# In-order ACT and DVE at the opening of the first feed-forward layer, and a new order of two tiles' steps

## The chip, the cores and the metric

The kernel runs on one core of a Trainium2 chip. The metric is the device time of one execution in microseconds (us). The core has a matrix engine (PE, with its weight loads shown apart as PEld), three engines for elementwise work (DVE, ACT, POOL) and SP, which issues the transfers. The engines run side by side. Each takes its own instructions in the order in which they were laid down, and they wait for each other by semaphores.

## The reference

One block works on 16 meta tokens and 1024 tokens of 1024 features in float32. A mixer (pooling and gated linear attention, merged by gates) is followed by a feed-forward part; what matters here is the end of the first and all of the second:

```
h = h + m @ w_out                                   # end of the mixer, m: the gated sum
u = rmsnorm(h, norm_ffn)
h = h + square(relu(u @ w_ff1)) @ w_ff2             # w_ff1: 1024 x 4096, w_ff2: 4096 x 1024
out = rmsnorm(h, norm_final)[:, 16:]
```

## The kernel before

**Products.** Every float32 operand is held as two float32r parts, high and low; a product is three matmuls (high x high, high x low, low x high: `mm3`, lines 246 to 248), each of 128 weights by 512 columns. The split of a weight block is a copy on ACT (L264, the high part) and a subtraction on DVE (L265, the low part), into one of four slots that go round.

**Quarters.** Both feed-forward layers save one product in eight by a Strassen scheme. In the first, `Quarters` takes the columns of `w_ff1` in 16 pairs of 128-column blocks. For pair i there are seven products, P1(i) to P7(i), each of four feature tiles by three matmuls, twelve matmuls in all. Their weights are blocks of `w_ff1` or sums of such blocks, made on DVE (`sums`, L315 for P5, L317 for P6, L319 for P7, L321 for P3); P1, P2 and P4 use blocks as they were loaded. Weights are made three products ahead of the product that uses them (`todo`); the blocks of pair i + 2 are loaded (L292) once P3(i)'s weights are made. The order of the products at the start is P1(0), P1(1), P2(0), P2(1), P5(0), P5(1), P6(0), P7(0), P4(0), P3(0), then P6(1), P1(2), P7(1), P5(2), P4(1), P2(2), P3(1) and so on (`order`). `run` is a generator: each step emits the weights three ahead, one product, and, after the next resume, what takes its result. P1 and P2 add into one bank of the `x` tag, whose copy after P1 is u2 (L361). P5 and P3 add into one bank of the `mm` tag; P6, P7 and P4 have an `ms` bank each. After P6, u2 is added (L369); after P7, u3 is made (L374) and the result A22 is taken from the P5 bank (L1494); P4 gives A12, and P3, added onto the P5 bank, gives A21. `ff_result` adds on DVE (L1494), then ACT does relu (L1496) and square (L1497), DVE forms sums (L1501 to L1509), and SP stores them (L1488).

**Moving operands.** The normalized tiles u, eight of 128 tokens, are transposed on PE and become seven operands. `turn_tile` does that for one tile: eight transposes into two banks, b[0] for the features 0 to 511 and b[1] for the rest (L1395). Tiles 0 to 3 give the operands of P1 and P2, and raw copies `lo` and `hi`, kept in `acc`. A tile t of 4 to 7 meets the copies of tile t - 4:

- `b12`, a copy of b[0] on ACT (L1404);
- `t1` = b[0] - lo on DVE (L1405), and its high part on ACT (L1406, `th`) and low part on DVE (L1407, `tl`): the operand of P5;
- both parts of b[1] (L1408, which calls L201 and L202): the operand of P3;
- lo = b[1] - t1, b12 = b[1] - b12, hi = hi - lo on DVE (L1409 to L1411), and both parts of the first two (L1414, L1415, tile `wo`): the operands of P6 and P7.

The operand of P4 is made of `hi` for all four column groups at once in `ff_room`: four copies on ACT (L1467, `t4h`) and four subtractions on DVE (L1468, `t4l`). After that `ff_room` gives the memory of `acc` to the results h.

**Order of the work.** `out_tile` multiplies one tile by a half of `w_out` in 24 matmuls, adds the residual (L1378), normalizes (`layer_norm`: ACT L234, L210, L212; DVE L211, L214, L218, L219, and L238, which writes u) and, between its two halves of matmuls, turns the tile of two steps earlier. The tiles come in the order 0, 4, 1, 5, 2, 3, 6, 7. So the last two, 6 and 7, are turned inside the first feed-forward layer, in `ff_layers`: tile 6 ahead of P1(1), tile 7 ahead of P2(1), and `ff_room` comes after P2(1). The first four weights are made ahead, in `ff_weights`.

PE's instructions keep the program's order throughout. Those of ACT, DVE and SP are placed by a scheduler that works with its own estimates of when operands are ready, except inside `in_order(True)` ... `in_order(False)`, where ACT's and DVE's keep the program's order among themselves. Instructions emitted outside such a section may still be placed between those inside. In the kernel before, such a section runs from the last part of the attention to `wo1_open`, ahead of `out_tile`; there is none in the stage of this change.

Of the kernel before, what the change touches and what calls it, by code (L numbers as in the profile page):

```python
# [11 lines left out]
ACT = mybir.ActivationFunctionType  # L12
ALU = mybir.AluOpType
# [92 lines left out]
def kernel(  # L106
# [10 lines left out]
    act, dve, pool, pe = nc.scalar, nc.vector, nc.gpsimd, nc.tensor  # L117
# [20 lines left out]
    def bank(tag):  # L138
        if tag in rota:
            turn_of[tag] = turn_of.get(tag, -1) + 1  # L140
            tag = rota[tag][turn_of[tag] % len(rota[tag])]
        return psp[tag].tile([P, 512], F32, name=f"b_{tag}", tag=tag)
# [48 lines left out]
    def f32(ap):  # L191
        return ap.bitcast(F32)
# [7 lines left out]
    def split_from_psum(hi, lo, ps):  # L200
        act.activation(hi, ps, ACT.Copy)  # L201
        dve.tensor_tensor(lo, ps, f32(hi), ALU.subtract)  # L202
# [47 lines left out]
    def quad(a):  # L250
        return a.rearrange("p (k c) -> p k c", k=4)
# [149 lines left out]
    S, rings = {}, [W1]  # L401

    def step(steps, fn, ring=None, aps=()):
        steps.append((ring, list(aps), fn))
# [38 lines left out]
    def halves():  # L443
        return [slice(h * HALF, (h + 1) * HALF) for h in range(2)]
# [28 lines left out]
    def v_tile(i, t, later=False):  # L473

        vw, w = S["vw"][i], 256 + 16 * (i == 0)
        if t == 8:
            half, at, n = 0, 0, META
        else:
            half, n = t // 4, P
            at = OFF[half] + (t % 4) * P  # L480
        b = bank("mm")[:n, :w]
        th, tl, hi, lo = TH[half][:, :, at : at + n], TL[half][:, :, at : at + n], vw[:, 0], vw[:, 1]
        if i == t == 0:

            for k in range(KT):
                pe.matmul(b, th[:, k], hi[:, k], start=k == 0, stop=False)
                pe.matmul(b, tl[:, k], hi[:, k], start=False, stop=False)
            for k in range(KT):
                pe.matmul(b, th[:, k], lo[:, k], start=False, stop=k == KT - 1)
        else:  # L490
            mm3(b, KT, lambda k: (th[:, k], tl[:, k]), lambda k: (hi[:, k], lo[:, k]))

        def leave():
            if t == 8:
                act.activation(vm[:, i * 256 : i * 256 + 256], b[:, :256], ACT.Copy)
            else:
                act.activation(S["v"][i][:, t], b[:, :256], ACT.Copy)

        def leave_lr():
            if i == 0:  # L500
                act.activation(S["lrtok"][:n, t], b[:, 256:], ACT.Copy)

        if later:
            return leave, leave_lr
        leave()
        leave_lr()
# [13 lines left out]
    def lr_turn():  # L520
        b = bank("ms")
        pe.transpose(b[:16, :16], S["lrtok"][:16, 8], ident[:16, :16])
        stacked(lrT_meta, b[:16, :16], 1)
        for h in range(2):
            b = bank("ms")
            for t in range(4):
                pe.transpose(b[:16, t * P : (t + 1) * P], S["lrtok"][:, 4 * h + t], ident)
            act.activation(gB[:16, h * HALF : (h + 1) * HALF], b[:16], ACT.Copy)
# [186 lines left out]
    def halved(p, j):  # L715

        h, l = gate_quarters.x[p] = [left.push(f"{p}{k}", [P, 4, HALF], F32R) for k in "hl"]
        for k in range(0, 4, 2):
            a = S["ut"][j][:, k : k + 2]
            act.activation(h[:, k : k + 2], a, ACT.Copy)  # L720
            dve.tensor_tensor(l[:, k : k + 2], a, f32(h[:, k : k + 2]), ALU.subtract)

    def differ(to, a, b):
        for k in range(0, 4, 2):
            to_, a_, b_ = (S["ut"][j][:, k : k + 2] for j in (to, a, b))
            dve.tensor_tensor(to_, a_, b_, ALU.subtract)

    def differences(run, values):


        b11, b21, b12, b22 = (0, 0), (0, 1), (1, 0), (1, 1)
        left.pop_to(S["left_x"])
        halved("P5", b11)
        for fn in values:
            fn()
        next(run)
        leave = v_tile(0, 8, True)
        differ(b11, b22, b11)
        next(run)
        for fn in leave:  # L740
            fn()
        halved("P6", b11)
        next(run)
        differ(b12, b22, b12)
        lr_turn()
        next(run)
        right.pop_to(S["right_ut"][4])
        halved("P7", b12)
        next(run)
        differ(b21, b21, b11)  # L750
        right.pop_to(S["right_ut"][2])
        halved("P4", b21)
        next(run)
        right.pop_to(S["right_ut"][0])
# [43 lines left out]
    one = []  # L798
# [212 lines left out]
    def in_order(on):  # L1011


        if on:
            S["order"] = tc.manual_schedule(engines={mybir.EngineType.Activation, mybir.EngineType.DVE})
            S["order"].__enter__()
        else:
            S.pop("order").__exit__(None, None, None)
# [344 lines left out]
    ORDER = (0, 4, 1, 5, 2, 3, 6, 7)  # L1363
# [18 lines left out]

        return fn

    def turn_tile(t, tags=("ms",)):

        u, acc, g = S["u2"][:, ORDER.index(t) % 2], S["acc"], t % 4
        cols, b = slice(g * P, (g + 1) * P), []  # L1390
        for j in range(2):
            turn_n[0] += 1
            b.append(quad(bank(tags[turn_n[0] % len(tags)])))
            for i in range(4):
                pe.transpose(b[j][:, i], u[:, (4 * j + i) * P : (4 * j + i + 1) * P], ident)  # L1395
        lo, hi = (quad(acc[:, g, c]) for c in halves())
        if t < 4:
            for j, raw_copy in enumerate((lo, hi)):
                k = slice(4 * j, 4 * j + 4)
                act.activation(raw_copy, b[j], ACT.Copy)  # L1400
                split_from_psum(MH[0][:, k, cols], ML[0][:, k, cols], b[j])
            return
        b12, t1 = (quad(acc[:, t, c]) for c in halves())
        act.activation(b12, b[0], ACT.Copy)  # L1404
        dve.tensor_tensor(t1, b[0], lo, ALU.subtract)  # L1405
        act.activation(MH[1][:, 0:4, cols], t1, ACT.Copy)  # L1406
        dve.tensor_tensor(ML[1][:, 0:4, cols], t1, f32(MH[1][:, 0:4, cols]), ALU.subtract)  # L1407
        split_from_psum(MH[1][:, 4:8, cols], ML[1][:, 4:8, cols], b[1])  # L1408
        dve.tensor_tensor(lo, b[1], t1, ALU.subtract)  # L1409
        dve.tensor_tensor(b12, b[1], b12, ALU.subtract)  # L1410
        dve.tensor_tensor(hi, hi, lo, ALU.subtract)  # L1411
        for n, a in enumerate((lo, b12)):
            fh, fl = (S["wo"][0][:, k, 4 * n : 4 * n + 4, cols] for k in range(2))
            act.activation(fh, a, ACT.Copy)  # L1414
            dve.tensor_tensor(fl, a, f32(fh), ALU.subtract)  # L1415

    for n, j in enumerate(YB[1]):
        if n < 2:
# [20 lines left out]
    for t in ORDER[:6]:  # L1439
        step(one, out_tile(t, 1))  # L1440
    step(one, lambda: ff_weights())
    for t in ORDER[6:]:
        step(one, out_tile(t, 1))

    def ff_weights():
        for n in range(4):
            ff_quarters.prime(n == 0)
        m = lambda half, j: tuple(t[half][:, 4 * j : 4 * j + 4] for t in (MH, ML))
        n = lambda j: tuple(S["wo"][0][:, k, 4 * j : 4 * j + 4] for k in range(2))
        ff_quarters.x = {"P1": m(0, 0), "P2": m(0, 1), "P5": m(1, 0), "P3": m(1, 1), "P6": n(0), "P7": n(1)}  # L1450
# [11 lines left out]
    def ff_room():  # L1462

        fh, fl = ff_quarters.x["P4"]
        for g in range(4):
            a, cols = quad(S["acc"][:, g, halves()[1]]), slice(g * P, (g + 1) * P)
            act.activation(fh[:, :, cols], a, ACT.Copy)  # L1467
            dve.tensor_tensor(fl[:, :, cols], a, f32(fh[:, :, cols]), ALU.subtract)  # L1468
        left.pop_to(S["left_acc"])
        S["h"] = left.push("h", [P, 2, 9, HALF], F32)  # L1470
        ff_quarters.room = True
# [165 lines left out]
    def ff_layers():  # L1637

        ff_open()
        del rota["mm"]  # L1640
        run = ff_quarters.run()
        for n in range(4):
            if n in (1, 3):
                turn_tile(ORDER[6 + n // 2])
            next(run)
        ff_room()
        for _ in run:
            pass

    for fn in (ff_layers, ff2_open, ff2):  # L1650
        step(one, fn)
# [47 lines left out]
```

## Time and profile before

| | us |
|---|---|
| median of 3 runs | 1238.97 (1238.19 to 1239.67) |
| the profiled execution, its own time | 1239.98 |
| span of its profile, first to last instruction | 1238.2 |
| first feed-forward layer, first to last product (about) | 617 to 930 of the span |

The page of the profile gives each engine's busy time, its share of the span and its count of instructions. A row of the timeline gives start, duration, engine, line, operation, output and inputs by the program's names, sizes and count; a bracket at its end gives the time that the engine sat idle before it and what released it. A row of the windows gives a stretch, its length and each engine's busy time with instruction counts, then the granted PE clock as a share of the full one, and the transfers. In the names, `b_mm`, `b_x` and `b_ms` are banks, `w1h` and `w1l` the parts of the weights, `th`, `tl`, `wo`, `t4h` and `t4l` parts of the moving operands. A queue of an engine is written with a q (SPq).

### The profile page before, as it was taken

What the parts mean: (1) busy time and instruction counts of PE and PEld (TensorE: products, weight loads), DVE (VectorE), ACT (ScalarE), POOL (GpSimd) and SP (SyncE); (2) the same over time, 40 slices, a digit from 0 to 9 for tenths busy, and PEclk for the clock granted to TensorE, in tenths of its full rate; (3) what the DMA queues carried; (4) which work ended last, traced back from release to release, by engine and by line L of the source; (5) the groups of instructions that cost most, each with busy time, mean ns of one, the idle gap of its engine ahead of it and who ended that gap; (6) DMA issues with size and microseconds to landing.
All of it is one profiled execution on the core that took longest, in us unless ns stands there. A gap on an engine that the chain in (4) does not pass through costs nothing.

```text
span 1238.2 us, 18288 instructions
## 1 busy us (share of the span) xinstructions
PE 1207.4 (98%) x6816; PEld 1006.6 (81%) x6816; DVE 852.3 (69%) x1388; ACT 618.3 (50%) x1099; POOL 66.3 (5%) x74
## 2 busy tenths in 40 slices
PE   7999999999999999899999999999999999999997
PEld 6978888888897778688878888888888888888886
DVE  5896676564456686633897776766775877887686
ACT  6677667322446664412664554545554444444554
POOL 2100000001101115400000000000000000000000
PEclk9999999999999999999999999999999999999999
DMA  8033326247102237741144444444559983333532
GB/s 250 2 96 117 111 85 186 61 139 235 35 19 78 69 120 247 264 127 51 70 137 152 164 155 141 158 149 162 162 198 322 342 268 102 94 97 100 162 97 90
DMA packets 142680, 173.84 MB, mean 140 GB/s; under 512 B 10968, under 2 KB 82416, under 8 KB 142592
## 3 DMA queue, kind: packets, MB, share of 16 engines
q1 hardware_dynamic: 142592, 172.68, 43.7%
q8 instruction: 53, 0.87, 0.3%
q14 instruction: 35, 0.29, 0.1%
HBM read 119.17 MB, written 53.48 MB: 139 GB/s over the span
## 4 chain that ended last, share of the span: by engine, by line
PE 87%; DVE 7%; ACT 3%; issue 1%; DMA 1%; SPq 0%; DVEq 0%; ACTq 0%
PE b_mm L246 10%; PE b_mm L247 10%; PE b_mm L248 10%; PE b_ms L248 9%; PE b_ms L246 9%; PE b_ms L247 9%; PE b_x L247 8%; PE b_x L246 8%; PE b_x L248 8%; PE b_sc L1147 1%; PE b_ms L550 1%; PE b_mx L246 1%; PE b_m L1249 1%; PE b_mx L248 1%; PE b_mx L247 1%
## 5 line engine op out<-in xcount | busy, mean ns | idle before, releaser
L246 PE MATMUL b_mm<-th,w1h 128*128 128x512 f32 (+1 forms) x312 | 117.7, 377 | 0.6 <-ACT th L1406 0.6
L247 PE MATMUL b_mm<-tl,w1h 128*128 128x512 f32 (+1 forms) x312 | 116.2, 372 | 0.6 <-DVE tl L1407 0.6
L248 PE MATMUL b_mm<-th,w1l 128*128 128x512 f32 (+1 forms) x312 | 116.0, 372 | 0.0
L246 PE MATMUL b_x<-th,w1h 128*128 128x512 f32 (+1 forms) x240 | 90.8, 378 | 0.0
L247 PE MATMUL b_x<-tl,w1h 128*128 128x512 f32 (+1 forms) x240 | 90.7, 378 | 0.0
L248 PE MATMUL b_x<-th,w1l 128*128 128x512 f32 (+1 forms) x240 | 90.4, 377 | 0.0
L264 ACT ACTIVATE w1h<-raw 128x512 fp32r<-128x512 f32 x96 | 59.5, 620 | 34.7 <-PE b_x L247 14.1
L265 DVE TENSOR_TENSOR w1l<-raw,w1h 128x512 fp32r<-128x512 f32 x96 | 65.7, 685 | 10.9 <-ACT w1h L264 10.9
L264 ACT ACTIVATE w1h<-fs 128x512 fp32r<-128x512 f32 x72 | 45.4, 630 | 46.2 <-PE b_ms L247 31.8
L246 PEld LDWEIGHTS b_mm<-th,w1h 128*128 128x128 f32 x312 | 58.6, 188 | 12.0 <-ACT th L1406 1.0
L247 PEld LDWEIGHTS b_mm<-tl,w1h 128*128 128x128 f32 x312 | 58.7, 188 | 10.6 <-DVE tl L1407 0.9
L248 PEld LDWEIGHTS b_mm<-th,w1l 128*128 128x128 f32 x312 | 58.7, 188 | 10.3
L264 ACT ACTIVATE w1h<-bt 128x512 fp32r<-128x512 f32 x44 | 27.8, 632 | 67.9 <-issue 63.6
L265 DVE TENSOR_TENSOR w1l<-fs,w1h 128x512 fp32r<-128x512 f32 x72 | 49.3, 686 | 14.7 <-ACT w1h L264 14.6
L1556 DVE TENSOR_TENSOR bt<-w,w 128x512 f32<-128x512 f32 x80 | 54.7, 684 | 1.1 <-DMA w<-in_w_ff_dram 1.1
L248 PEld LDWEIGHTS b_x<-th,w1l 128*128 128x128 f32 x240 | 45.2, 188 | 8.4
L246 PEld LDWEIGHTS b_x<-th,w1h 128*128 128x128 f32 x240 | 45.1, 188 | 8.4
L247 PEld LDWEIGHTS b_x<-tl,w1h 128*128 128x128 f32 x240 | 45.1, 188 | 8.2
L264 ACT ACTIVATE fxh<-bt 128x512 fp32r<-128x512 f32 x36 | 22.8, 632 | 54.9 <-issue 49.2
L247 PE MATMUL b_ms<-wo,w1h 128*128 128x512 f32 x128 | 49.8, 389 | 0.0
L248 PE MATMUL b_ms<-wo,w1l 128*128 128x512 f32 x128 | 49.8, 389 | 0.0
L246 PE MATMUL b_ms<-wo,w1h 128*128 128x512 f32 x128 | 49.8, 389 | 0.0
(446 smaller groups left out, 3373.9 us busy)
## 6 DMA issues: line engine op xcount, KB each, us to landing
hf_dram<-h SPq DMA_DIRECT2D x112, 256.0 KB, 2.1
raw<-hf_dram SPq DMA_DIRECT2D x112, 256.0 KB, 2.7
w<-in_w_ff_dram SPq DMA_DIRECT2D x64, 256.0 KB, 4.7
raw<-in_w_in_dram SPq DMA_DIRECT2D x24, 512.0 KB, 4.8
raw<-in_w_ff_dram SPq DMA_DIRECT2D x16, 512.0 KB, 4.1
rawx<-in_w_ff_dram SPq DMA_DIRECT2D x16, 512.0 KB, 4.2
xs<-in_x_dram SPq DMA_DIRECT2D x8, 512.0 KB, 4.6
rawx<-in_w_in_dram SPq DMA_DIRECT2D x8, 512.0 KB, 4.6
```

Of the source, the lines that this page charges most:

```text
L246: pe.matmul(ps, ah, bh, start=first and i == 0, stop=False, skip_group_check=more)
L247: pe.matmul(ps, ah, bl, start=False, stop=False, skip_group_check=more)
L248: pe.matmul(ps, al, bh, start=False, stop=last and i == n - 1, skip_group_check=more)
L264: act.activation(hi, a, ACT.Copy)
L265: dve.tensor_tensor(lo, a, f32(hi), ALU.subtract)
L550: pe.transpose(b[j][:, i], u[:, (4 * j + i) * P : (4 * j + i + 1) * P], ident)
L1147: pe.matmul(b[to, e, j], kk[r, s], qq[r, s], start=True, stop=True, tile_position=(e * CH, u * CH))
L1249: pe.matmul(o[part(u), e, j], scc[part(u), e, j], v[part(u), j, e], start=j == 0, stop=False, tile_position=(u * CH, u * CH), skip_group_c ...
L1556: dve.tensor_tensor(bt, w, S["w2"][q[3:]][:, i], ALU.add if q[2] == "+" else ALU.subtract)
```

## The change

In `turn_tile`, for tiles 4 to 7, the copy b12 moves behind the operands of P5 and P3. The difference steps go into a function of their own, which is called at once, or, if a list `later` is given, put off. An in-order section begins after `ff_weights`, ahead of the w_out products of tiles 6 and 7, and ends after P3(0). In `ff_layers` tile 7 is turned ahead of P2(0), not P2(1); both tiles' difference steps come ahead of P2(1); `ff_room` comes after P5(0).

```diff
-    def turn_tile(t, tags=("ms",)):
+    def turn_tile(t, tags=("ms",), later=None):
...
         b12, t1 = (quad(acc[:, t, c]) for c in halves())
-        act.activation(b12, b[0], ACT.Copy)
         dve.tensor_tensor(t1, b[0], lo, ALU.subtract)
         act.activation(MH[1][:, 0:4, cols], t1, ACT.Copy)
         dve.tensor_tensor(ML[1][:, 0:4, cols], t1, f32(MH[1][:, 0:4, cols]), ALU.subtract)
         split_from_psum(MH[1][:, 4:8, cols], ML[1][:, 4:8, cols], b[1])
-        dve.tensor_tensor(lo, b[1], t1, ALU.subtract)
-        dve.tensor_tensor(b12, b[1], b12, ALU.subtract)
-        dve.tensor_tensor(hi, hi, lo, ALU.subtract)
-        for n, a in enumerate((lo, b12)):
-            fh, fl = (S["wo"][0][:, k, 4 * n : 4 * n + 4, cols] for k in range(2))
-            act.activation(fh, a, ACT.Copy)
-            dve.tensor_tensor(fl, a, f32(fh), ALU.subtract)
+        act.activation(b12, b[0], ACT.Copy)
+
+        def differences():
+            dve.tensor_tensor(lo, b[1], t1, ALU.subtract)
+            dve.tensor_tensor(b12, b[1], b12, ALU.subtract)
+            dve.tensor_tensor(hi, hi, lo, ALU.subtract)
+            for n, a in enumerate((lo, b12)):
+                fh, fl = (S["wo"][0][:, k, 4 * n : 4 * n + 4, cols] for k in range(2))
+                act.activation(fh, a, ACT.Copy)
+                dve.tensor_tensor(fl, a, f32(fh), ALU.subtract)
+
+        if later is None:
+            differences()
+        else:
+            later.append(differences)
...
     step(one, lambda: ff_weights())
+    step(one, lambda: in_order(True))
     for t in ORDER[6:]:
         step(one, out_tile(t, 1))
...
         run = ff_quarters.run()
-        for n in range(4):
-            if n in (1, 3):
-                turn_tile(ORDER[6 + n // 2])
+        later = []
+        for n in range(5):
+            if n in (1, 2):
+                turn_tile(ORDER[5 + n], later=later)
+            elif n == 3:
+                for fn in later:
+                    fn()
             next(run)
         ff_room()
+        for _ in range(5):
+            next(run)
+        in_order(False)
         for _ in run:
             pass
```

The new lines shift the numbers. In the new kernel t1 is L1404, its parts L1405 and L1406, the copy b12 L1408, the differences L1411 to L1413 and their parts L1416 and L1417; the operand of P4 is made at L1475 and L1476, the additions of `ff_result` stand at L1502, relu and square at L1504 and L1505, the stores at L1496.

## The prediction

> **What bounds the kernel now.** The page comes first, then TensorE's own waits, then four stretches of the stage that the change touches.
>
> ```profile
> span 1238.2 us, 18288 instructions
> PE 1207.4 (98%) x6816; PEld 1006.6 (81%) x6816; DVE 852.3 (69%) x1388; ACT 618.3 (50%) x1099; POOL 66.3 (5%) x74
> ```
>
> ```profile
> PE b_mm L247 <- DVE tl L1407: 0.6, 1, 0.6
> PE b_mm L246 <- ACT th L1406: 0.6, 1, 0.6
> PE b_ms L1395 <- DVE small L211: 0.5, 1, 0.5
> ```
>
> ```profile
> 620.00:625.00 5.00, 5.00 (x28) 4.23 (x27) 4.49 (x11) 3.75 (x9) 0.00 (x0) 1.00 0.55 189
> 625.00:630.00 5.00, 5.00 (x28) 4.07 (x26) 5.00 (x9) 2.90 (x6) 0.00 (x0) 1.00 0.33 105
> 630.00:635.00 5.00, 3.80 (x16) 2.70 (x15) 5.00 (x10) 3.37 (x6) 0.00 (x0) 1.00 0.00 0
> 635.00:640.00 5.00, 5.00 (x24) 4.15 (x23) 5.00 (x9) 3.55 (x7) 0.00 (x0) 1.00 0.29 96
> ```
>
> TensorE (PE) is busy 98% of the span. The second block lists the waits of the stage, 1.7 us of them; the columns of the third are length, then busy time of PE, PEld, DVE, ACT and POOL, granted clock, DMA share, GB/s. From 625 to 640 DVE is busy in all of its 15 us. So PE bounds the kernel, and in this stage DVE stands right behind it: PE can move forward only as far as DVE delivers.
>
> ```profile
> 629.86 0.39 PE L248 MATMUL b_x<-th,w1l 128*128 128x512 f32 x1
> 630.82 0.50 PE L246 MATMUL b_mm<-th,w1h 128*128 128x512 f32 x1 [0.57 <-ACT th L1406]
> 631.95 0.50 PE L247 MATMUL b_mm<-tl,w1h 128*128 128x512 f32 x1 [0.63 <-DVE tl L1407]
> 632.29 0.40 PE L248 MATMUL b_mm<-th,w1l 128*128 128x512 f32 x1
> ...
> 637.34 0.39 PE L246 MATMUL b_ms<-wo,w1h 128*128 128x512 f32 x1
> 637.57 0.39 PE L247 MATMUL b_ms<-wo,w1h 128*128 128x512 f32 x1
> ...
> 642.78 0.39 PE L246 MATMUL b_ms<-t4h,w1h 128*128 128x512 f32 x1
> ...
> 645.53 0.47 PE L246 MATMUL b_mm<-th,w1h 128*128 128x512 f32 x1
> ```
>
> Matmuls start 0.227 us apart (637.34, 637.57; 24 of them take 642.78 - 637.34 = 5.44), so a product of twelve takes 2.73. P2(1) ends with the first row. P5(0) was due at 629.86 + 0.23 = 630.09; it waits for both parts of tile 7's operand. P6(0) begins at 637.34 instead of 630.09 + 5.44 = 635.53, so the two waits with their restarts cost 1.8 us. P4(0) begins at 642.78, P3(0) at 645.53.
>
> **The change, part by part.** Line numbers are those of the kernel before. Removed: the 1.8 us. In the new order of instructions tile 7's transposes stand one product earlier on PE, and its operand for P5(0) before the difference steps. What is late next follows from the new queues of ACT and DVE, walked with the durations of these rows:
>
> ```profile
> 613.75 0.22 DVE L214 SCALAR_TENSOR_TENSOR small<-small 128x1 f32<-128x1 f32 x1
> 614.39 1.29 DVE L238 SCALAR_TENSOR_TENSOR u<-acc,small,gB 128x1024 f32<-128x1024 f32 x1
> 615.59 0.68 DVE L202 TENSOR_TENSOR tl<-b_ms,th 128x512 fp32r<-128x512 f32 x1
> ...
> 617.59 0.69 DVE L1378 TENSOR_TENSOR acc<-b_mm,acc 128x512 f32<-128x512 f32 x1 [0.40 <-PE b_mm L248]
> 618.19 0.68 DVE L315 TENSOR_TENSOR fs<-raw 128x512 f32<-128x512 f32 x1
> ...
> 636.02 0.69 DVE L265 TENSOR_TENSOR w1l<-fs,w1h 128x512 fp32r<-128x512 f32 x1
> ...
> 644.09 0.69 DVE L265 TENSOR_TENSOR w1l<-raw,w1h 128x512 fp32r<-128x512 f32 x1 [0.42 <-ACT w1h L264]
> 644.70 0.68 DVE L1494 TENSOR_TENSOR h<-b_mm,u3p 128x512 f32<-128x512 f32 x1
> ```
>
> ```profile
> 618.64 1.05 ACT L234 ACTIVATE u<-acc 128x1024 f32<-128x1024 f32 x1
> ...
> 620.14 0.20 ACT L212 ACTIVATE small<-small 128x1 f32<-128x1 f32 x1
> ...
> 636.14 1.09 ACT L1496 ACTIVATE h<-b_x 128x512 f32<-128x512 f32 x2 [0.34 <-DVE t4l L1468]
> 637.11 1.15 ACT L1497 ACTIVATE h<-h 128x512 f32<-128x512 f32 x2
> ...
> 643.42 0.63 ACT L264 ACTIVATE w1h<-raw 128x512 fp32r<-128x512 f32 x1 [2.76 <-DMA raw<-in_w_ff_dram]
> ```
>
> Two prices come out of them. A 512-column DVE step holds the queue for 0.60 us (617.59 to 618.19). Where DVE makes a value, ACT copies its high part, and DVE subtracts for the low part, DVE's second step stands 0.69 + 0.04 + 0.67 = 1.40 after its first (643.42 to 644.09 is the 0.67), and DVE idles 0.8 unless other work stands between. I call this a round trip. Before, the scheduler put other work there. In order, almost none stands there.
>
> 1. Tile 7's norm. ACT's Square (L234) no longer stands behind two t4h copies and starts at 618.31, not 618.64. To the end of L212 are 1.70 (618.64 to 620.34), L214 to L238 are 0.64, L238 holds 1.20: DVE is free at 621.9.
> 2. Tile 6: t1, round trip, two low parts, the sum of P5(0), round trip, its low part: 1.40 + 0.60 + 0.60 + 1.40 + 0.60 = 4.6. Free at 626.5.
> 3. Tile 7 with the sum of P5(1): 4.6 again. Its P5 operand is whole at 628.6, before 630.09: the old waits are gone. Free at 631.1. The weights' low part for P5(1), at 631.2, is in time for its product at 632.8.
> 4. The difference steps of both tiles: ten DVE steps, 6.0. Free at 637.1. The ACT copies fit between.
> 5. P6(0): its sum at 637.1, high part at 638.5, low part 639.2. PE is due at 635.53 and **waits 3.0 us**, first for ACT's high part (L264). That is 1.2 later than before, 1.4 with the restart.
> 6. DVE: P7(0)'s sum and round trip to 641.1, then all four t4l steps (before, two of them stood ahead of the turns), ending at 643.6. The relu and square steps of pairs 0 and 1 write where these read (the row at 636.14 shows that wait). In order they stand ahead of P4(0)'s weight copy on ACT; before, they stood behind it. Two of each took 2.12 (636.14 to 638.26); alternating, each square waits for its relu: 2.3. So L264 for P4(0) starts at 645.9 and its low part ends at 647.3. PE, due at 638.5 + 5.44 + 0.35 (restart and late low part) = 644.3, **waits 2.3 us**, to 646.6.
> 7. P3(0) adds onto the bank that still holds P5(0), so it needs DVE's A22 addition (L1494) done; before, that stood at 644.70, just ahead of 645.53. In the new queue nine DVE steps stand from P4(0)'s low part to it, among them P5(2)'s sum (L315). This one was emitted after the in-order section and was placed in front of the u3p and A22 additions. It reads a block whose load is issued only after P4(0)'s low part, 647.3. The price of that added wait:
>
> ```profile
> 638.65 1.18 SPq L292 DMA_DIRECT2D raw<-in_w_ff_dram  x2
> DMA to landing us min/median/max: 4.0/4.2/6.0
> ```
>
> The nearest row is the same pair of loads: issued at 638.65, used at 643.42, 4.77 later. I take 4.75 and keep 4.0 and 6.0. Then L315 at 652.1, low part 652.7, u3p 653.3, P3(1)'s sum 653.9, A22 at 654.5 to 655.2, and P3(0) starts at 655.25. Due at 646.6 + 2.73 + 0.3 = 649.6, PE **waits 5.6 us**. With 4.0 it is 654.5, with 6.0 656.5. With no wait for the load, L315 stands at 650.4, its successor waits for ACT to 651.2, and P3(0) starts at 653.75. Behind L315 stand the next low part, both additions, and ACT's relu for them.
>
> Against 645.53 the shift is **9.7 us** (8.2 to 11.0); nothing behind it is idle, so it stays. The other edits cost nothing: the turns of tiles 4 and 5 move their b12 copy behind the P5 parts, and PE has products of w_out over them; without that cover each is one copy from a bank, 0.55 (half of 1.09). Tile 3's second low part now stands ahead of an addition; that delays the wait of 0.5 at L1395 by about 0.1. SP issues the two loads in swapped order and two later ones some places further back, where a pair lasts 19 us (84 matmuls of 0.227).
>
> **The clock.** A wait in an earlier stage shows what follows it:
>
> ```profile
> 77.74 0.54 PE L248 MATMUL b_ms<-P4h,w1l 128*128 128x512 f32 x1 [1.80 <-DVE w1l L265]
> ...
> 79.36 0.63 PE L246 MATMUL b_ms<-P4h,w1h 128*128 128x512 f32 x1
> 79.79 0.63 PE L247 MATMUL b_ms<-P4l,w1h 128*128 128x512 f32 x1
> ```
>
> ```profile
> 74.65:78.06 3.41, 1.61 (x6) 0.86 (x5) 3.41 (x5) 2.69 (x5) 0.00 (x0) 1.00 0.43 154
> 78.06:81.48 3.42, 3.42 (x9) 2.65 (x8) 3.23 (x6) 0.00 (x0) 0.00 (x0) 0.50 0.93 221
> 402.33:405.74 3.41, 1.78 (x10) 1.16 (x9) 3.30 (x6) 0.89 (x2) 1.65 (x1) 1.00 0.13 17
> ```
>
> A 3.41 us stretch with PE busy 1.61 was followed by one at half the clock, matmuls 0.43 apart; one with 1.78 busy was not. [...] A whole slow stretch runs 8 matmuls where 15 fit, 8 x 0.20 = 1.6 us; from half a stretch to one and a half, 0.8 to 2.4. A drop after the first wait is swallowed by the second and third. I add 1.6. [...]
>
> **Sum.** 9.7 + 1.6 = 11.3 us. On the profiled execution: span 1238.2 to 1249.5, its own time 1239.98 to 1251.3, 1.0 above the median. On the median of 1238.97: 1250.3.
>
> **The rivals.**
> - No clock drop: the third wait ends as a slow stretch would have ended, or a longer gap is needed. For it: waits of 0.57 and 0.63 did nothing here. Against: 1.80 did. 9.7 us, 1248.7.
> - Only P6(0) is late. P4(0)'s copy would have to start by 641.7 and A22 end by 647, over 4 us ahead of my walk. For it: both came in time before. Against: ACT's place behind the relus, and the new queue of DVE. 1.4 us, 1240.4.
> - Not slower: the round trips cost no DVE time. Five stand ahead of P6(0)'s low part, 0.8 idle each, 4.0 in all; without 3.0 of it P6(0) is in time. For it: in the old order DVE ran 15 us without idle time. Against: in order, what stands between the two halves of a trip is mostly what waits for the same copy. Only the removed 1.8 is left: 1237.2.
>
> **How the numbers follow.** Forecast 0.82, no drop 0.11, only P6(0) 0.03, not slower 0.04. The forecast's bounds are 8.2 + 0.8 = 9.0 to 11.0 + 2.4 = 13.4, the first rival's low end 8.2: 1247.2 to 1252.4, with half a microsecond for the measurement 1246.5 to 1253.0. A measurement of this kernel tells about 0.2%, 2.5 us, from no change. The last two rivals lie within it; faster by more would need over 2.5 us where the stage's waits with restarts hold some 2.3. Faster 0.01, same 0.06, slower 0.93.
>
> **What would show it.** Right: no wait of b_mm for th or tl of tile 7; in their place PE waits of about 3 us for P6(0)'s high weights, 2.3 for P4(0)'s, over 5 for P3(0) behind DVE's A22 addition; DVE idle gaps of 0.8 between 622 and 639; a granted clock of 0.50 for some 3.4 us after 655. Wrong: DVE without gaps there, an A22 addition ahead of 650, or PE idle under 5 us in all from 630 to 660. Then I mispriced the round trips or the load.

## The result and the profile after

| | before | changed |
|---|---|---|
| median, us | 1239.54 (5 runs, 1238.19 to 1239.90) | 1250.44 (5 runs, 1249.02 to 1251.11) |
| ratio | | 1.0088, 95% interval 1.0074 to 1.0101 |
| profiled execution: own time, span | 1239.98, 1238.2 | 1251.11, 1249.3 |

The changed kernel is 10.9 us slower; 11.3 were forecast. First the page's head and the waits of PE in the changed kernel (total, times, longest):

```profile
span 1249.3 us, 18284 instructions
PE 1209.8 (97%) x6816; PEld 1006.5 (81%) x6816; DVE 852.4 (68%) x1388; ACT 618.5 (50%) x1099; POOL 66.2 (5%) x74
```

```profile
PE b_mm L246 <- DVE h L1502: 5.0, 1, 5.0
...
PE b_ms L246 <- ACT w1h L264: 3.6, 2, 2.8
...
PE b_mm L246 <- DVE c L761: 1.1, 1, 1.1
```

DVE and ACT are as busy as before, to 0.2 us; there is no more work, only more waiting. The two waits for `th` and `tl` of tile 7 are gone. In their place stand 5.0 us for A22's addition and 3.6 in two waits for ACT's weight copies. (The third row belongs to an earlier stage; it comes up again at the end.) The same stretches as before, and the ones behind them:

```profile
625.00:630.00 5.00, 5.00 (x23) 4.10 (x23) 3.18 (x5) 3.15 (x6) 0.00 (x0) 1.00 0.01 2
630.00:635.00 5.00, 5.00 (x24) 4.14 (x23) 4.80 (x8) 1.87 (x4) 0.00 (x0) 1.00 0.00 0
635.00:640.00 5.00, 2.17 (x6) 1.21 (x6) 3.79 (x7) 1.75 (x4) 0.00 (x0) 0.85 0.00 0
640.00:645.00 5.00, 5.00 (x20) 4.03 (x19) 3.10 (x5) 3.89 (x8) 0.00 (x0) 0.81 0.00 0
645.00:650.00 5.00, 3.90 (x15) 2.28 (x13) 2.84 (x5) 1.97 (x4) 0.00 (x0) 1.00 0.55 180
650.00:655.00 5.00, 0.29 (x1) 0.32 (x2) 3.43 (x6) 1.03 (x2) 0.00 (x0) 0.71 0.51 134
655.00:660.00 5.00, 5.00 (x15) 3.93 (x15) 2.71 (x5) 3.16 (x6) 0.00 (x0) 0.61 0.28 105
```

DVE, busy in all 15 us from 625 to 640 before, is now busy in 3.18 + 4.80 + 3.79 = 11.8 of them, and that is where the loss begins. PE does not notice until 635; it runs dry there, for a moment near 646, and again at 650. The granted clock, the third column from the end, dips twice. The timeline of PE, with the matmuls that waited:

```profile
635.06 0.39 PE L248 MATMUL b_mm<-th,w1l 128*128 128x512 f32 x1
638.28 0.65 PE L246 MATMUL b_ms<-wo,w1h 128*128 128x512 f32 x1 [2.83 <-ACT w1h L264]
...
646.42 0.50 PE L246 MATMUL b_ms<-t4h,w1h 128*128 128x512 f32 x1 [0.81 <-ACT w1h L264]
...
649.33 0.39 PE L248 MATMUL b_ms<-t4h,w1l 128*128 128x512 f32 x1
654.71 0.77 PE L246 MATMUL b_mm<-th,w1h 128*128 128x512 f32 x1 [5.00 <-DVE h L1502]
...
659.50 0.39 PE L246 MATMUL b_ms<-wo,w1h 128*128 128x512 f32 x1
```

P5(1)'s last matmul starts at 635.06. P6(0) starts at 638.28, P4(0) at 646.42, P3(0) at 654.71 and P6(1), at the end of these rows, at 659.50. DVE's timeline shows why:

```profile
621.65 0.68 DVE L1404 TENSOR_TENSOR acc<-b_ms,acc 128x512 f32<-128x512 f32 x1
623.04 0.69 DVE L1406 TENSOR_TENSOR tl<-acc,th 128x512 fp32r<-128x512 f32 x1 [0.70 <-ACT th L1405]
...
626.24 0.68 DVE L1404 TENSOR_TENSOR acc<-b_ms,acc 128x512 f32<-128x512 f32 x1
...
630.81 0.68 DVE L1411 TENSOR_TENSOR acc<-b_ms,acc 128x512 f32<-128x512 f32 x1
...
636.82 0.68 DVE L317 TENSOR_TENSOR fs<-fs,raw 128x512 f32<-128x512 f32 x1
638.25 0.69 DVE L265 TENSOR_TENSOR w1l<-fs,w1h 128x512 fp32r<-128x512 f32 x1 [0.76 <-ACT w1h L264]
...
646.40 0.69 DVE L265 TENSOR_TENSOR w1l<-raw,w1h 128x512 fp32r<-128x512 f32 x1 [3.00 <-ACT w1h L264]
...
651.47 0.69 DVE L315 TENSOR_TENSOR fs<-raw 128x512 f32<-128x512 f32 x1 [1.13 <-DMA raw<-in_w_ff_dram]
...
653.88 0.68 DVE L1502 TENSOR_TENSOR h<-b_mm,u3p 128x512 f32<-128x512 f32 x1
```

One round trip is seen whole: t1 at 621.65, its low part 1.39 later, 0.70 of it idle. Each tile takes 4.6 (621.65, 626.24, 630.81), the ten difference steps 6.0 (to 636.82). Behind P4(0)'s low part at 646.40 the A22 addition comes only at 653.88.

### The profile page after: what moved, and what is told of

It reads as the page before. It is cut to its first block, busy times and chain, and to the rows that moved or that the text cites. A ratio compares the mean times of both kernels' runs of the same rounds, so it can differ in the third digit from the quotient of the medians.

```text
span 1249.3 us, 18284 instructions
## 1 busy us (share of the span) xinstructions
PE 1209.8 (97%) x6816; PEld 1006.5 (81%) x6816; DVE 852.4 (68%) x1388; ACT 618.5 (50%) x1099; POOL 66.2 (5%) x74
## 4 chain that ended last, share of the span: by engine, by line
PE 85%; DVE 8%; ACT 3%; DMA 1%; issue 1%; POOL 0%; SPq 0%; DVEq 0%; ACTq 0%
PE b_mm L246 10%; PE b_mm L247 10%; PE b_mm L248 10%; PE b_ms L246 9%; PE b_ms L247 9%; PE b_ms L248 9%; PE b_x L246 8%; PE b_x L247 8%; PE b_x L248 8%; PE b_sc L1147 1%; PE b_ms L550 1%; PE b_mx L246 1%; PE b_m L1249 1%; PE b_mx L248 1%; PE b_mx L247 1%
```

## The experiments

All are compared with the kernel before, run on the same chip. Beside the medians stands a time from each trace, which is one execution of the kernel: from P1(0)'s first matmul to the start of the last matmul, 612.83 us before (617.38 to 1230.22) and 624.22 with the change (617.14 to 1241.36), 11.4 more. It leaves out the front of the program, which no edit touches and which moves by some 2 us between executions (P1(0) begins between 615.3 and 617.6).

| run | median, us | kernel before, us | ratio (95% interval) | trace stretch against before |
|---|---|---|---|---|
| x1_free | 1238.53 | 1239.44 | 0.9988 (0.9980 to 0.9997) | -1.2 |
| x2_section_only | 1247.52 | 1239.44 | 1.0066 (1.0051 to 1.0082) | +8.0 |
| x3_short_section | 1242.76 | 1239.44 | 1.0024 (1.0015 to 1.0033) | +4.2 |
| x4_filled | 1243.08 | 1239.44 | 1.0027 (1.0017 to 1.0037) | +3.3 |
| x5_late_relu | 1248.43 | 1239.68 | 1.0071 (1.0054 to 1.0088) | +7.9 |
| x6_long_section | 1251.16 | 1239.68 | 1.0094 (1.0079 to 1.0108) | +11.2 |
| x7_busy_wait | 1248.59 | 1239.68 | 1.0078 (1.0061 to 1.0095) | +9.6 |
| x8_b12_only | 1238.15 | 1239.68 | 0.9987 (0.9978 to 0.9995) | -1.4 |
| x9_filled_late | 1243.39 | 1240.02 | 1.0025 (1.0015 to 1.0034) | +2.2 |
| x10_filled_short | 1240.36 | 1240.02 | 1.0004 (0.9995 to 1.0014) | +0.6 |

### The two halves of the change: x1 and x2

x1, against the changed kernel:

```diff
-    step(one, lambda: in_order(True))
...
-        in_order(False)
```

> The changed kernel with its new emission order (tile 7 turned ahead of P2(0), differences put off, b12 later), but without the in-order section. Theory (the loss is the section's: ACT and DVE in program order leave DVE idle in round trips and put the relus and the A22 addition badly): the scheduler fills the trips again, none of the three new PE waits is there, and of the old 1.3 us of waits for tile 7's operand at most 0.4 is left: 0.7 to 1.5 us below the kernel before. Rival (the stage has simply more to do ahead of P6(0) in the new place of the steps, whoever orders it): P6(0) still waits, 3 us or more above the kernel before.

The median is 0.9 us below the kernel before, and the interval is clear of 1. In the trace DVE is filled again and PE waits for nothing from 625 to 645; one wait of 0.26 us, for tile 7's u, is left.

```profile
625.00:630.00 5.00, 5.00 (x23) 4.13 (x22) 4.93 (x9) 3.71 (x7) 0.00 (x0) 1.00 0.25 80
630.00:635.00 5.00, 5.00 (x23) 4.13 (x22) 5.00 (x9) 3.73 (x6) 0.00 (x0) 1.00 0.00 0
635.00:640.00 5.00, 5.00 (x23) 4.10 (x22) 5.00 (x10) 3.16 (x6) 0.00 (x0) 1.00 0.31 83
```

So the new places of the steps, b12's among them, are good for about 1 us, and the whole loss is the section's. The rival falls.

x2, against the kernel before:

```diff
     step(one, lambda: ff_weights())
+    step(one, lambda: in_order(True))
...
         ff_room()
+        for _ in range(6):
+            next(run)
+        in_order(False)
```

> The kernel before with the in-order section of the changed kernel (from ff_weights to P3(0)), and nothing else changed. Theory (the section costs, not the new places): waits of 2 to 3 us each ahead of P5(0), P4(0) and P3(0), 8 to 10 us above the kernel before. Rival (the new places cost): within 3 us of the kernel before.

The median is 8.1 us above. PE's waits in the trace:

```profile
628.22 0.50 PE L246 MATMUL b_x<-th,w1h 128*128 128x512 f32 x1 [1.89 <-ACT u2p L361]
643.40 0.80 PE L246 MATMUL b_ms<-wo,w1h 128*128 128x512 f32 x1 [2.41 <-ACT w1h L264]
652.39 0.47 PE L246 MATMUL b_mm<-th,w1h 128*128 128x512 f32 x1 [1.77 <-DVE h L1495]
```

The size was expected rightly, the places were not: the first wait is not P5(0)'s but P2(1)'s, for the copy of u2 out of the bank onto which P2(1) adds, and the second, behind the twelve matmuls of P6(0), is P7(0)'s, not P4(0)'s. What holds is that the section alone costs 8 us, with the old places too. With the new ones it costs more: 11.4 + 1.2 = 12.6 us between the traces of x1 and the change.

### Where the section costs: x3, x4, x5, x6

x3, against the changed kernel:

```diff
         ff_room()
+        in_order(False)
         for _ in range(5):
             next(run)
-        in_order(False)
```

> The changed kernel with the section ended right after ff_room instead of after P3(0). Theory: the first wait (P6(0), some 3 us) stays, since its queue is the same; the relus and the A22 addition are free to go behind P4(0)'s copy and ahead of P5(2)'s sum, so the waits at P4(0) and P3(0) are under 1 us together: 2.5 to 4 us above the kernel before, the upper end if the clock drops after the first wait with no later wait to swallow it. Rival (all three waits are one late chain that begins with P6(0)): still over 8 us above.

The median is 3.3 us above (4.2 in the trace). The first wait stays and the others do not arise. The row of the windows, with its granted clock of 0.54, shows what the first wait costs when no later one follows:

```profile
638.25 0.79 PE L246 MATMUL b_ms<-wo,w1h 128*128 128x512 f32 x1 [2.80 <-ACT w1h L264]
```

```profile
640.00:645.00 5.00, 5.00 (x14) 3.93 (x13) 4.91 (x9) 4.51 (x9) 0.00 (x0) 0.54 0.75 202
```

Counted from P1(0), P6(0) starts 1.1 us later than before. From there to P4(0) it takes 8.67 us (638.25 to 646.92) where it took 5.44, so the slow clock, granted at 0.50 from 637.75 to 644.57, costs some 3 us more. The waits at P4(0) and P3(0) are thus no mere consequence of a late P6(0): two thirds of the loss is made behind `ff_room`.

x4, against the changed kernel, with `parts` holding the old body of the loop:

```diff
         def forms(self):
-            for p, i, s in ahead(self.sums(), self.lead):
-                yield p, i, split(s)
...
+            made = []
+            for x in self.sums():
+                made.append(x)
+                if len(made) > self.lead:
+                    yield from self.parts(*made.pop(0))
+            for x in made:
+                yield from self.parts(*x)
...
         run = ff_quarters.run()
+        ff_quarters.lead = 1
```

> The changed kernel, section and all, with the sums of the weights emitted one form ahead of the splits, so that one sum stands in each split's round trip on DVE. DVE's number of steps is the same. Theory (the idle time of round trips delays P6(0)): P6(0)'s wait shrinks to under 2 us in all, P4(0)'s to about 1 and P3(0)'s to about 2; 2.5 to 5 us above the kernel before. Rival (DVE has too much work there, idle time or not): 9 us or more above, as with the change.

The median is 3.6 us above. DVE has the same steps and the section is in force, but from 625 to 640 DVE is busy for 14.05 us, where it was 11.8 with the change:

```profile
625.00:630.00 5.00, 5.00 (x23) 4.10 (x23) 4.20 (x7) 3.22 (x6) 0.00 (x0) 1.00 0.01 3
630.00:635.00 5.00, 5.00 (x24) 4.14 (x23) 5.00 (x10) 2.47 (x5) 0.00 (x0) 1.00 0.00 0
635.00:640.00 5.00, 3.80 (x16) 2.50 (x15) 4.85 (x9) 3.23 (x6) 0.00 (x0) 1.00 0.00 0
```

PE's waits shrink from 2.83, 0.81 (an estimated 2.3 without the slow clock) and 5.00 to these:

```profile
637.38 0.50 PE L248 MATMUL b_ms<-wo,w1l 128*128 128x512 f32 x1 [1.08 <-DVE w1l L265]
...
643.60 0.50 PE L246 MATMUL b_ms<-t4h,w1h 128*128 128x512 f32 x1 [0.93 <-ACT w1h L264]
...
648.62 0.47 PE L246 MATMUL b_mm<-th,w1h 128*128 128x512 f32 x1 [1.73 <-DVE h L1510]
```

It was idle time between DVE's steps, not their number. (L1510 is this kernel's A22 addition.) No clock row from 620 to 645 is below 1.00 here, and behind 648.62 the matmuls start 0.23 us apart.

x5, against the changed kernel:

```diff
         ff_room()
-        for _ in range(5):
+        ff_quarters.room = False
+        for n in range(5):
+            ff_quarters.room = n > 1
             next(run)
```

> The changed kernel, but ff_quarters.room is set only after two of the five products behind ff_room, so the relus and squares of pairs 0 and 1 are emitted behind the weights of P4(0) and P3(0). Theory (the second wait is ACT's: P4(0)'s copy behind the relus; the third is DVE's A22 addition in its queue): P4(0)'s wait goes, P6(0)'s stays at 3, and P3(0), due some 2 us earlier, waits again, 4 to 5 us, since the A22 addition and the load come only some 2.5 us earlier: 6.6 without, about 8 with the clock drop above the kernel before. Rival (P3(0) is late only because P4(0) was): P3(0)'s wait under 2 us, 5 us above or less.

The median is 8.8 us above (7.9 in the trace).

```profile
638.76 0.50 PE L246 MATMUL b_ms<-wo,w1h 128*128 128x512 f32 x1 [2.84 <-ACT w1h L264]
...
652.02 0.47 PE L246 MATMUL b_mm<-th,w1h 128*128 128x512 f32 x1 [2.96 <-DVE h L1502]
```

The wait at P4(0) is gone: it was the relus' place on ACT. P3(0)'s was expected at 4 to 5 and is 2.96, because the clock dropped after the first wait (0.95 from 635 to 640, 0.71 from 640 to 645) and PE came later; the total is as expected. That P3(0) still waits speaks against the rival.

x6, against the changed kernel:

```diff
         ff_room()
-        for _ in range(5):
+        for _ in range(6):
             next(run)
```

> The changed kernel with the section one product longer, so that P5(2)'s sum (the DVE step that waits for a load) comes behind the A22, A12 and A21 additions. Theory (the load is a small part of the third wait; the queue of weight forms ahead of the additions is the rest): the third wait falls from 5.0 to about 4, and about as much is given back at a weight wait some 12 us later: 10 to 11 us above the kernel before. Rival (the load wait is what makes P3(0) late): third wait under 1 us, 6 us above or less.

The median is 11.5 us above (11.2 in the trace), no better than the change and a little more than expected.

```profile
654.17 0.76 PE L246 MATMUL b_mm<-th,w1h 128*128 128x512 f32 x1 [4.03 <-DVE h L1502]
```

```profile
650.00:655.00 5.00, 0.97 (x3) 0.77 (x3) 3.27 (x6) 1.54 (x3) 0.00 (x0) 0.80 0.59 160
655.00:660.00 5.00, 5.00 (x13) 3.85 (x13) 3.26 (x6) 2.13 (x4) 0.00 (x0) 0.52 0.28 105
```

The load is 1.0 of the third wait's 5.0, as the theory had it, and the rest stays without it. Where the 1.0 went was a miss: no later weight wait took it. The clock did. It is granted at 0.50 for 6.83 us in both traces (652.12 to 658.95 with the change, 653.01 to 659.84 here). But P3(0) starts earlier here, so PE is busy for 5.67 us of the slow time instead of 4.24 (hence 0.52 in the last row and 0.61 with the change). Of the 1.0, 0.2 is left in the trace.

### The clock: x7

36 transposes that nothing reads, ahead of P3(0) of the first layer:

```diff
+                if (p, i) == ("P3", 0) and self is ff_quarters:
+                    idle = bank("ms")
+                    for _ in range(36):
+                        pe.transpose(idle[:, :P], ident, ident)
                 more = p in ("P2", "P3")
```

> The changed kernel with 36 transposes of the identity matrix ahead of P3(0), into a bank that nobody reads, so PE is busy for about 3.6 of the 5 us of its third wait. Nothing else moves. Theory (the third wait costs 1.6 us more by the clock that follows it): no stretch of half clock behind 655, P3(0) starts when it does in the changed kernel; 1.6 us (0.8 to 2.4) below the changed kernel. Rival (the slow stretch is hidden, or comes anyway after the first two waits): as the changed kernel, 11 us above.

The median is 8.9 us above the kernel before, where the change is 10.9 above; the trace has 1.8 less than that of the change.

```profile
648.58 4.09 PE L360 MATMUL b_ms<-ident 128*128 128x128 f32 x36
653.87 0.47 PE L246 MATMUL b_mm<-th,w1h 128*128 128x512 f32 x1 [1.19 <-DVE h L1506]
...
656.70 0.39 PE L246 MATMUL b_ms<-wo,w1h 128*128 128x512 f32 x1
```

```profile
655.00:660.00 5.00, 5.00 (x24) 4.12 (x23) 4.59 (x8) 3.83 (x8) 0.00 (x0) 1.00 0.28 105
```

P3(0) starts 37.7 us after P1(0) here and 37.6 with the change, so the delay is the same; but the clock stays at 1.00, and P3(0) takes 2.83 (653.87 to 656.70), where it took 4.79 (654.71 to 659.50) with the change. So the trace shows the clock's share: 1.96 us. Work that does nothing made the changed kernel faster there. By the medians alone that would not be safe: the two intervals overlap (1.0061 to 1.0095, 1.0074 to 1.0101), and one of x7's four runs took 1251.78 us.

### The edit that was costed at nothing: x8

Against the kernel before:

```diff
-        act.activation(b12, b[0], ACT.Copy)
         dve.tensor_tensor(t1, b[0], lo, ALU.subtract)
...
         split_from_psum(MH[1][:, 4:8, cols], ML[1][:, 4:8, cols], b[1])
+        act.activation(b12, b[0], ACT.Copy)
```

> The kernel before, with one part of the change: for tiles 4 to 7 the copy b12 on ACT behind the operands of P5 and P3. No section, the old places. The prediction costed this edit at nothing. Theory (ACT's copy b12 stands ahead of the high part that P5(0) waits for, in tile 7's chain): the wait for the high part goes and of 1.2 us at P5(0) some 0.3 is left: 0.7 to 1.2 us below the kernel before. Rival (it changes nothing that PE waits for): within 0.3 us.

The median is 1.5 us below, a little more than expected, and the interval is clear of 1. The wait for the high part is gone, 0.19 of the other is left:

```profile
628.56 0.50 PE L247 MATMUL b_mm<-tl,w1h 128*128 128x512 f32 x1 [0.19 <-DVE tl L1406]
```

### The cures together: x9 and x10

x9 has the edits of x4 and x5, x10 those of x4 and x3.

> The changed kernel with two cures at once: sums one form ahead (a sum in each split's round trip) and the relus of pairs 0 and 1 behind the weights of P4(0) and P3(0). Theory (three separate causes in the two queues, so cures add as far as PE waits allow): no wait at P4(0), under 2 us at P6(0), about 2 at P3(0); 2 to 3.7 us above the kernel before, the upper end if the clock drops. Rival (the cures are the same gain twice): as with the filled trips alone, 3.3 us above in the stretch from P1(0) to the last matmul, with P4(0)'s wait still there.

> The changed kernel with the sums one form ahead and the section ended right after ff_room. Theory (with the trips filled the first wait is small, and without the section behind ff_room the second and third do not arise): P6(0) waits 1.2 to 1.8 us in all, P4(0) under 0.7; 0 to 1.5 us above the kernel before. Rival (in-order ACT and DVE cost the stage more than round trips and these two placings): 3 us or more above.

x9 is 3.4 us above by the medians and 2.2 in the trace. x10 is 0.3 above, and its interval holds 1. The waits of x9:

```profile
PE b_mm L246 <- DVE h L1510: 2.0, 1, 2.0
PE b_ms L248 <- DVE w1l L265: 1.1, 1, 1.1
```

Those of x10:

```profile
PE b_ms L248 <- DVE w1l L265: 1.1, 1, 1.1
...
PE b_mm L246 <- DVE h L1510: 0.5, 1, 0.5
```

In x9 P4(0)'s wait is gone as well, but P3(0)'s grows from 1.73 to 2.0, so the cures add only in part. Its medians do not tell it from x4 (1243.08, 1243.39); the gain of 1.2 stands in the two traces alone. In x10 the section, kept short and with its trips filled, costs nothing that can be measured against the kernel before; against x1, which has no section, its trace is still 1.7 us longer.

Of all, x1 and x8 beat both kernels. x1 contains the edit of x8, and its gain is no larger (1.2 and 1.4 us in the traces). So with the section away, tile 7's earlier turn and the put-off difference steps add nothing that can be measured to the move of b12.

## Why the prediction was right

- **The removed waits** are gone, as said. But part of them needed no section and no new place: moving b12 alone (x8) takes 1.4 of the 1.8 us in the trace. The prediction costed that edit at nothing for tiles 4 and 5 and did not look at what it does for tile 7.
- **Steps 1 to 4**, DVE's queue: free at 621.9, 626.5, 631.1 and 637.1 in the working; in the trace at 621.65, 626.24, 630.81 and 636.82. All are 0.25 to 0.3 early, as P1(0) itself is by 0.24. DVE's idle gaps in the round trips are 0.70 to 0.76, not 0.8, but the distance of 1.40 between the steps, on which the walk rests, is 1.39 in the trace.
- **Step 5**: 3.0 us at P6(0), measured 2.83. x4 shows the cause, the round trips.
- **Step 6**: P4(0) at 646.6, measured 646.42; P4(0)'s copy stood behind the relus, and x5 shows that without them it does not wait. The wait itself was 0.81 instead of 2.3 because the clock dropped after the first wait and the second swallowed it, as the prediction said it would.
- **Step 7**: 5.6 us at P3(0), measured 5.00. The term that was mis-sized is the load, 4.75 from issue to use; this trace has 4.35:

```profile
647.12 1.01 SPq L292 DMA_DIRECT2D raw<-in_w_ff_dram  x2
```

  Used at 651.47. P3(0) stands 654.71 - 645.53 = 9.2 us later than before (9.4 from P1(0)) instead of 9.7.
- **The clock**: 1.6 taken, 0.8 to 2.4 kept; 4.79 - 2.83 = 1.96 measured, 9.2 + 1.96 = 11.1 is the whole difference of the two spans. That the third wait would drop the clock was the author's estimate, from the drop behind the wait of 1.80 us; the rows around P3(0)'s start have 0.71 and 0.61. The clock was slow until some 4 us after P3(0)'s start, not 3.4: it was granted at 0.50 from 652.12 to 658.95, the first 2.6 us of that inside the wait. It dropped behind the first wait of 2.83 us too: the row from 635 to 640 has 0.85 and the next 0.81.
- **The rivals**: no drop is refuted by the 0.61 and by x7; only P6(0) late, by the rows at 646.42 and 654.71, and x3 shows where that case lies, 3.3 above and not 1.4, since that rival left the clock out. Not slower was about idle time in the trips: x4 shows that filling them takes two thirds of the price away (3.6 us above instead of 10.9), but the change does not fill them.
- **The sum** came closer than its terms: the shift was 0.3 to 0.5 us smaller than taken and the clock 0.4 larger. That these two nearly cancel is luck; the mechanism is not. (The stated range is a little wide of its own terms: 1247.2 - 0.5 is 1246.7, not 1246.5.)
- **Not settled**: how the third wait's remaining 4.0 us divide among the eight other DVE steps ahead of A22. Of the 7.48 us from P4(0)'s low part (646.40) to A22 (653.88), DVE is idle for 0.76 in a round trip and 1.13 for the load; the rest is steps one behind the other. x5 and x6 take only one cause away each.

## What to carry to other kernels

Before an engine is held to the program's order, walk its new queue: every value that one engine makes, another copies and the first takes up again costs the first an idle round trip (1.39 us here, 0.7 of it idle) unless the written order puts other work into it. A wait of the matrix engine is paid twice where the clock falls behind it (5.00 us of wait and 1.96 of slow clock here), so price the wait and the slow stretch, and ask whether a later wait swallows the stretch. And test the parts of a change alone: here the smallest part held the gain, another the loss, and the rest nothing that could be measured.

## What the runs showed of the hardware

The clock's answer to one and the same wait differs between executions. In the earlier stage both kernels wait 1.8 us for P4's low weights. Before, the clock dropped there (PEclk 0.81 and 0.85). With the change, in an unaltered stage, it did not:

```profile
75.00:80.00 5.00, 2.60 (x10) 1.80 (x10) 5.00 (x9) 1.15 (x3) 0.00 (x0) 1.00 0.89 245
80.00:85.00 5.00, 4.75 (x21) 3.96 (x22) 3.58 (x7) 4.12 (x8) 0.00 (x0) 1.00 0.27 70
```

Instead PE waits 1.1 us more a little later, for `c` (L761, the third row of the waits above), where it did not wait before. So a wait of 1.8 us was followed by a drop in one trace and by none in the other; what decides between the two was not shown. x2 has both answers within one stage: behind its wait of 1.89 us the clock dropped (matmuls 0.43 apart from 629.86 to 632.42), behind that of 1.77 us it did not (0.23 apart from 652.70 on). The longer waits of the changed kernel, 2.83 and 5.00, were each followed by a drop (rows of 0.85 and 0.81, 0.71 and 0.61).
